# A seven-product output projection for the pooling layer, four units at a time

## The chip, the cores and the metric

The kernel runs on one core of a Trainium2 chip. The metric is the device time of one execution in microseconds (us); lower is better. A time is the median of several executions. The profile is one more execution, recorded by the hardware profiler. PE is the matrix engine, PEld its loading of weights, DVE the vector engine, ACT the scalar engine, POOL the general engine, and SP the queue that issues every transfer here.

## The reference, cut to what matters

Two pre-norm residual layers over 4096 tokens of width 1024: first sliding-window attention, then a pooling mixer. The change lies in the second, apart from the preparation of its weights.

```python
def pool_layer(h, w_in, w_mix, scale, w_out):
    u, z = jnp.split(h @ w_in, [POOL_WIDTH], axis=-1)
    p = multiscale_pool(u)       # trailing means over 2/4/8/16 tokens, minus u
    m = jnp.einsum('bsgc,gcd->bsgd', p, w_mix).reshape(B, S, POOL_WIDTH) * scale
    return (m * jax.nn.silu(z)) @ w_out

# x = x + pool_layer(rmsnorm(x)); the result is rmsnorm(x, final_g)
```

## The kernel before, in words

Every fp32 matrix product is made of three passes: each factor is split into a high and a low part (`split_sb`, L133 on ACT and L134 on DVE; the high part is a rounded copy, the low part the difference), and high*high, high*low and low*high are added up in PSUM (`PASSES`). A product of 128 contracted rows, 128 output channels and 512 tokens is thus three matmuls.

**Stage A (attention)** goes over eight blocks of 512 tokens (`s` = 0 to 7; the last outputs run on into the start of what follows). Beside it, in blocks 2 to 7, four calls of `seven` per block (half a weight unit each) prepare the weights of the pooling layer: for `u` and `z` units they make the seven weight combinations of a two-by-two block product, split them and store them to HBM (`w7_...`); for the output units `o` they only split the weight and store it in four pieces (`wo_...`). One such half costs seven splits of 128x256, seven stores and four sums on POOL for `u` and `z`, and four splits and four stores for `o`. Their order is u, z, o for each of the four units, so that blocks 2 and 5 hold four of the first kind and blocks 3, 4, 6 and 7 two of each.

**Stage B (pooling)** goes over four groups `g` of 1024 tokens. Each has an in-phase and an out-phase.

The in-phase makes eight units of 256 channels (u3, z3, u2, z2, ... u0, z0) by a two-by-two block scheme with seven products in place of eight: the token halves t and the channel halves k of each pair `p` give the right-hand factors B11, T1, T2, T3, B21, B22, T4 (`factor_sum` makes the T by differences in place, `factor` splits the result into a `set_...` tile). One `product` is 12 matmuls (four pairs, three passes) over 512 tokens and needs one weight tile of 512 KB, `w7_load`. Five such tiles are in flight. Four products of a unit add up in one PSUM bank X, one after the other; ACT copies the bank to the tile `ct_...` after each stage (`snapshot`, L656; the last is `result`, L662) before the next product may write it, and DVE adds the banks Y and Z (L660). So the order within a unit is 1, (3 of the unit before), 6, 5, 7, 2, 4.

A finished `u` unit goes through `pooled` (L710, L715: one to four shifted sums and a difference), a finished `z` unit through `gated`: z + z*tanh(z/2) on ACT (L721) and DVE (L722), times half the pooled value (L723). The results lie in four `raw` tiles `ar`, one for each pair.

The out-phase takes them directly: for each pair the four quarters B11, B12, B21, B22 are split, and each of four units (o3 to o0) is four calls of `o_pair` with 24 matmuls each (two channel halves, two token halves, two contracted halves, three passes) into four PSUM banks. That is 96 matmuls per unit and 384 per group. `o_result` adds the bank to the residual x (L694, the residual loaded to a `ct` tile by `o_open` in two transfers of 512 KB per unit), squares it (L734) and adds up the squares (L735); `stored` writes the unit to HBM in one transfer of 1 MB. The next group's x is loaded meanwhile (`h_load`, tile `xr`), scaled and made into factors.

The final normalisation of a group runs piece by piece in the in-phase of the next: `final_piece` loads 256 KB (`fin`), scales it on DVE (L788) and stores it, 16 times. In the last group it happens at the end: the last unit is computed in three parts (`LASTP`: token half 0, then two quarters of token half 1), each normalised as it is done (`last_sum`, `last_rsqrt`, `last_spread`, `last_scale`).

What issues when is written out by hand: every step is an event with a planned time (`at(t, fn, ...)`), counted in product lengths (`PROD` = 2.73 us). Events are emitted in the order of time; in stage B the compiler's scheduler may still move an instruction ahead of one that is not ready by its own estimate. Each engine then works strictly in its order, and SP issues the transfers in its own order: a transfer that has to wait for a free buffer or for DVE holds up those behind it.

Of the kernel before, what the change touches and what calls it, by code (L numbers as in the profile page):

```python
# [20 lines left out]
G = 512  # L21
# [31 lines left out]
def trunk_kernel(ctx, tc, xt, xm, ng, w_a_in, sinks, w_a_out, wu_t, wmix, pscale, w_b_z, w_b_out, fg, out):  # L53
# [17 lines left out]
    wout = {}  # L71
# [447 lines left out]
    def seven_load(key, src, hf):  # L519
        if hf == 0 and key[0] == "o":  # L520
            wout[key[1]] = [dram.tile([128, 2, 2, UC], F32, name=f"wo_{key[1]}_{i}") for i in range(4)]
        elif hf == 0:
            wseven[key] = [dram.tile([128, 2, 2, 2, 128], F32, name=f"w7_{key[0]}{key[1]}_{i}") for i in range(7)]
# [5 lines left out]
    def seven(key, hf):  # L529
        raw = wraws.pop((key, hf))  # L530
        if key[0] == "o":
            for c in range(4):
                t = lp.tile([128, 2, UC], F32R, tag="sl", bufs=SLOTS["sl"], name=f"part_o{key[1]}_{hf}_{c}")
# [25 lines left out]
    PROD, PAIR = 2.73, 5.45  # L559
# [6 lines left out]
    def open_left():  # L566
        left.close()
        for name, kw in (("bl", {}), ("bp", dict(space=PSUM))):
            pl[name] = E(tc.tile_pool(name=name, bufs=1, side="left", reuse_waits="tile", **kw))
        pl["ucar"] = pl["bl"].tile([128, 4, 2, 16], F32, name="ucar")  # L570
# [3 lines left out]
        for j, w in enumerate(WINDOWS):  # L574
            for t in range(w - 1):
# [4 lines left out]
              setl=("bl", 8), ct=("bl", 2), wk=("bl", 1), th=("bl", 1), sq=("bl", 1), sr=("bl", 2), sl=("bl", 1),  # L580
# [17 lines left out]
    def factor_sum(g, name, p):  # L598
        ph = (g, "in")
# [14 lines left out]
    def factor(ph, name, p):  # L614
        late = p < 2 if ph[1] == "out" else name in ("T4", "B22")
        t = bt([128, 2, G], "setl" if late else "set", f"set_{ph[0]}{ph[1]}_{name}_{p}", F32R)
# [7 lines left out]
    def w7_load(u, i):  # L624
        src = wout[u[2]][i] if u[1] == "o" else wseven[u[1], u[2]][i - 1]
# [4 lines left out]
    def product(u, i):  # L630
        bank = {1: "X", 6: "X", 7: "X", 4: "X", 2: "Y", 5: "Z", 3: "Z"}[i]
        first = i in (1, 2, 5)
        if first:
            banks[u, bank] = bpsum(bank, f"{bank}_{u[0][0]}{u[1]}{u[2]}")
        ps, w = banks[u, bank], w7.pop((u, i))
        for a, p in enumerate(PAIRS):
            t = sets[u[0], RIGHT[i], p]
            for b, (wl, hl) in enumerate(PASSES):
                nc.tensor.matmul(ps, w[:, p // 2, wl, p % 2], t[:, hl], start=(first and a == 0 and b == 0),  # L639
# [25 lines left out]
    def o_open(u):  # L665
        g, j = u[0][0], u[2]
        if g < NP - 1:
            c = bt([128, 2, 16 + G2], "ct", f"ct_{g}o{j}")[:, :, 16:]
        else:
            c = bt([128, 2, G2], "raw", f"ct_{g}o{j}")  # L670
        cts[u] = c
        for t in range(2):
            nc.sync.dma_start(c[:, :, G * t:G * t + G], x1[2 * g + t][j])

    def o_rhs(u, p, k, hl, t):
        return sets[u[0], f"B{k + 1}{t + 1}", p][:, hl]

    def o_pair(u, a):
        p = PAIRS[a]
        if a == 0:  # L680
            for i, tag in enumerate(("X", "Y", "Z", "pt")):
                banks[u, i] = bpsum(tag, f"{tag}_{u[0][0]}o{u[2]}")
        w = w7.pop((u, p))
        for i in range(4):
            n, t = i // 2, i % 2
            for k in range(2):
                for b, (wl, hl) in enumerate(PASSES):
                    nc.tensor.matmul(banks[u, i], w[:, wl, k, 128 * n:128 * n + 128], o_rhs(u, p, k, hl, t),
                                     start=(a == 0 and k == 0 and b == 0), stop=(a == 3 and k == 1 and b == 2))

    def o_result(u, i):
        n, t = i // 2, i % 2
        b = blk(u, n, t)
# [301 lines left out]
    for g in range(NP):  # L995
# [92 lines left out]
        if g == NP - 1:  # L1088
            continue
# [75 lines left out]
```

## Time and profile before

| | |
|---|---|
| median of 3 runs | 2626.57 us (2622.93 to 2632.19) |
| profiled execution | 2624.14 us, span 2622.0 us |
| PE busy | 2535.1 us, 97% of the span |
| DVE busy | 1504.4 us, 57% |
| ACT busy | 1041.8 us, 40% |
| POOL busy | 580.8 us, 22% |
| moved by DMA | 626.05 MB, mean 239 GB/s |

The time of the profiled execution lies 2.1 us above its span; the span is what the views of the trace divide. Stage B begins at 1619.4 us. A row of a window gives, for each engine, its busy time and (x) its instructions, then the granted PE clock (1.00 is full speed), the mean busy share of the 16 DMA engines and the rate.

### The profile page before, as it was taken

Reading aid. Unit: us, or ns where it says so; the run is one execution under the profiler, and the core shown is the slowest. Engines: PE = TensorE matmul, PEld = TensorE weight load, DVE = VectorE, ACT = ScalarE, POOL = GpSimd, SP = SyncE. Lnnn points to the kernel's source line nnn. Section 1 sums busy time; section 2 is a strip of 40 time slices with the busy share of each in tenths; the row PEclk is TensorE's granted clock in tenths of the full one; section 3 lists DMA queues with packets and bytes.
Section 4 is the critical chain, followed back from the end, with each engine's and each line's share of the span. In section 5 each row is a group of like instructions: output and inputs, shape, how many; then the busy total and the mean of one; then the engine's idle time right before and its main releaser. Section 6 shows DMA issues by size and latency. Waiting matters only on the chain.

```text
span 2622.0 us, 34809 instructions
## 1 busy us (share of the span) xinstructions
PE 2535.1 (97%) x12604; PEld 2135.6 (81%) x12604; DVE 1504.4 (57%) x2281; ACT 1041.8 (40%) x2680; POOL 580.8 (22%) x883
## 2 busy tenths in 40 slices
PE   6999999999999999999999999999999999999997
PEld 5888888888888888888888887888877877887886
DVE  5366656466466466565565557546646655655544
ACT  4464544455454454554554543222313231332221
POOL 3553323343243334333333330000000000000000
PEclk9998999999999999999999999999999999999999
DMA  8853856877767867877767758666677668758752
GB/s 293 307 200 129 304 190 206 292 251 242 265 239 245 288 230 238 295 242 232 271 234 247 250 196 301 193 216 244 203 257 268 217 225 279 258 177 279 247 203 97
DMA packets 175191, 626.05 MB, mean 239 GB/s; under 512 B 23198, under 2 KB 33438, under 8 KB 145324
## 3 DMA queue, kind: packets, MB, share of 16 engines
q1 hardware_dynamic: 175020, 623.83, 70.2%
q8 instruction: 100, 1.64, 0.2%
q14 instruction: 71, 0.58, 0.1%
HBM read 489.47 MB, written 117.51 MB: 231 GB/s over the span
## 4 chain that ended last, share of the span: by engine, by line
PE 65%; DMA 18%; DVE 10%; ACT 3%; issue 2%; POOL 1%; SPq 1%; DVEq 0%; POOLq 0%; ACTq 0%
PE mm L278 25%; PE s L395 3%; DMA fin<-x 2%; PE mm L288 2%; PE X_0u L639 2%; DMA out<-fin 2%; PE X_0z L639 2%; PE po L449 1%; PE X_1u L639 1%; DMA xt<-in_xt 1%; PE pT L420 1%; PE X_1z L639 1%; DMA rsq<-rs 1%; DMA w<-wparts 1%; PE X_3u L639 1%
## 5 line engine op out<-in xcount | busy, mean ns | idle before, releaser
L278 PE MATMUL mm<-h,w 128*128 128x512 f32 x3456 | 846.0, 396 | 8.0 <-DVE sz L364 3.4
L278 PEld LDWEIGHTS mm<-h,w 128*128 128x128 f32 x3456 | 638.7, 190 | 136.6 <-DVE sz L364 3.9
L278 PE MATMUL mm<-a,w 128*128 128x512 f32 x1536 | 375.8, 395 | 8.6 <-DMA w<-wparts 8.5
L436 POOL TENSOR_SCALAR_AFFINE_SELECT m<-m 64x256 fp32r<-64x256 f32 x512 | 230.7, 451 | 587.5 <-ACT m L427 502.0
L278 PEld LDWEIGHTS mm<-a,w 128*128 128x128 f32 x1536 | 282.8, 189 | 67.5 <-DMA w<-wparts 10.6
L407 ACT ACTIVATE P<-s,mx 128x129 f32<-128x129 f32 x512 | 182.0, 370 | 112.0 <-DVE mx L404 109.8
L412 POOL TENSOR_TENSOR P<-P,sm 128x516 f32<-128x516 f32 x128 | 145.7, 1139 | 154.3 <-DVE sm L411 142.9
L766 POOL TENSOR_TENSOR rs<-ms,mhalf 128x4 f32<-128x4 f32 x7 | 7.0, 1007 | 743.0 <-DVE ms L765 743.0
L456 ACT COPY tmp<-po 64x256 f32<-64x256 f32 x256 | 94.2, 368 | 145.6 <-PE po L450 87.7
L395 PEld LDWEIGHTS s<-kt,q 128*128 128x128 f32 x1024 | 134.4, 194 | 14.7 <-ACT s L386 4.8
L457 DVE TENSOR_TENSOR o<-po,tmp 64x256 f32<-64x256 f32 x256 | 107.7, 421 | 58.8 <-ACT tmp L456 53.0
L395 PE MATMUL s<-kt,q 128*128 128x192 f32 x1024 | 138.0, 276 | 2.8 <-ACT s L386 1.9
L327 DVE SCALAR_TENSOR_TENSOR q<-mm,q 64x512 fp32r<-64x512 f32 x128 | 88.2, 689 | 76.6 <-ACT q L326 74.9
L326 ACT ACTIVATE q<-mm 64x512 fp32r<-64x512 f32 x128 | 75.8, 593 | 74.7 <-PE mm L278 44.9
L407 ACT ACTIVATION_READ_ACCUMULATOR P<-s,mx 128x1 f32 x512 | 104.6, 204 | 0.0
L428 DVE TENSOR_TENSOR m<-pT,m 128x512 fp32r<-128x512 f32 x128 | 87.7, 685 | 26.9 <-ACT m L427 26.0
L400 DVE COPY_PREDICATED s<-mask,s 128x256 f32<-128x256 int8 x128 | 54.3, 424 | 74.6 <-PE s L395 67.9
L288 PE MATMUL mm<-w,h 128*128 128x256 f32 x768 | 96.4, 284 | 0.0
L288 PEld LDWEIGHTS mm<-w,h 128*128 128x128 f32 x768 | 94.9, 193 | 0.5
L427 ACT CAST m<-pT 128x512 fp32r<-128x512 f32 x128 | 75.0, 586 | 42.1 <-PE pT L420 39.0
L404 DVE TENSOR_REDUCE mx<-s 128x4 f32<-128x516 f32 x128 | 88.7, 693 | 3.3
L788 DVE SCALAR_TENSOR_TENSOR fin<-fin,fg_sb,bco 128x512 f32<-128x512 f32 x48 | 36.0, 751 | 88.6 <-DMA fin<-x 86.5
(357 smaller groups left out, 4342.7 us busy)
## 6 DMA issues: line engine op xcount, KB each, us to landing
w<-wparts SPq DMA_DIRECT2D x196, 1024.0 KB, 6.6
wparts<-w SPq DMA_DIRECT2D x28, 1024.0 KB, 6.8
xt<-in_xt SPq DMA_DIRECT2D x32, 512.0 KB, 6.1
res<-in_xt SPq DMA_DIRECT2D x32, 512.0 KB, 7.3
x<-res SPq DMA_DIRECT2D x32, 512.0 KB, 10.2
xr<-x SPq DMA_DIRECT2D x32, 512.0 KB, 5.5
xm<-in_xm SPq DMA_DIRECT2D x28, 512.0 KB, 7.0
w_u<-part_u SPq DMA_DIRECT2D x56, 256.0 KB, 3.0
```

Of the source, the lines that this page charges most:

```text
L278: nc.tensor.matmul(ps[:, c], w[:, wl, k % 4, 128 * c:128 * c + 128], rhs(k, hl), start=(k == 0 and i == 0), stop=(k == NK - 1 and i == 2))
L288: nc.tensor.matmul(ps[:, b], hts[s, k][:, hl, 128 * b:128 * b + 128], wtiles[U, k // 4][:, wl, k % 4], start=(k == 0 and i == 0), stop=(k ...
L327: nc.vector.scalar_tensor_tensor(dst[64 - r:128 - r], src, -SCALE, f32(dst[r:r + 64]), op0=ALU.mult, op1=ALU.subtract)
L395: nc.tensor.matmul(ps[:, 2 * c + u, 2 - 2 * u:194 - 2 * u], qs[s, j][:, c, 2 * b + u].rearrange("p r x -> p (r x)"), kt[:, j, hl, t:t + 19 ...
L404: nc.vector.tensor_reduce(mx.rearrange("p (c u) -> p c u", c=2), view(ps, 1, [(512, 2), (319, 2), (1, 129)]), axis=AX.X, op=ALU.min)
L407: nc.scalar.activation(P[:, i, 0:129], view(ps, 1 + 512 * (i // 2) + 319 * (i % 2), [(1, 129)]), AF.Exp, bias=mx[:, i:i + 1], scale=-1.0, ...
L412: nc.gpsimd.tensor_mul(P[:, :, 0:129], P[:, :, 0:129], sm.unsqueeze(2).to_broadcast([128, 4, 129]))
L428: nc.vector.tensor_sub(m1[:, 1], pv, f32(m1[:, 0]))
L436: nc.gpsimd.affine_select(out=v[rows], in_=f32(mu[wr, u, l]).rearrange("p c (r q) -> p c r q", r=2), **after)
L456: nc.scalar.copy(tmp[d:d + 64], pv[e:e + 64, r])
L457: nc.vector.tensor_add(dst, pv[d:d + 64, r], tmp[d:d + 64])
L639: nc.tensor.matmul(ps, w[:, p // 2, wl, p % 2], t[:, hl], start=(first and a == 0 and b == 0), stop=(a == 3 and b == 2), skip_group_check= ...
```

## The change

1. The output units are made by the seven-product scheme too. `seven` prepares `o` like `u` and `z`; `o_pair` and `o_result` go. Each unit is seven calls of `product`, so a group's out-phase has 4 x 7 x 12 = 336 matmuls of 512 tokens.
2. All four output units go through the products together: 1 for o3, o2, o1, o0, then 2 for all four, then 5, 6, 7, 3, 4 (in the last group 1, 6, 5, 7, 3, 2, 4). The banks X and Z of the four units take the tags X, Y, Z and pt. DVE adds each bank to the residual directly (`o_add`, seven times per unit), so the residual must be there in four blocks by channel half and token half (`o_load`, 16 transfers of 256 KB; `o_store`, 16 of 256 KB).
3. The out-phase needs B11, T1, T2, T3, B21, B22, T4 of each pair: seven splits and four differences where there were four splits. Tables of planned times (`OUT_FACTORS`, `IN_FACTORS`, `LAST_FACTORS`) place them and the factors of the next group.
4. The in-phase takes u and z of a pair together, product by product: 1u 1z 6u 6z 5u 5z 7u 7z 2u 2z 3u 3z 4u 4z.
5. The gate uses the function SiLU on ACT and one product on DVE in place of Tanh and two operations.
6. Loads and stores of stage B that are not weights are tied behind the last weight load in SP's order (`behind_w7`).
7. The new tail: token half 1 is finished first and normalised under the remaining products; the last product (4) of token half 0 is done in two quarters of 256 tokens, each for all four units.

The diff, cut:

```diff
@@ seven_load, seven
-        if hf == 0 and key[0] == "o":
-            wout[key[1]] = [dram.tile([128, 2, 2, UC], ...) for i in range(4)]
-        elif hf == 0:
+        if hf == 0:
             wseven[key] = [dram.tile([128, 2, 2, 2, 128], ...) for i in range(7)]
...
-        if key[0] == "o":
-            for c in range(4):
-                t = lp.tile([128, 2, UC], F32R, tag="sl", ...)
-                split_sb(t[:, 0], t[:, 1], raw[:, c])
-                nc.sync.dma_start(wout[key[1]][2 * hf + c // 2][:, :, c % 2], f32(t))
-            return
@@ buffers
-              setl=("bl", 8), ct=("bl", 2), wk=("bl", 1), ...
+              setl=("bl", 8), ct=("bl", 3), wk=("bl", 1), ...
@@ factor
-        late = p < 2 if ph[1] == "out" else name in ("T4", "B22")
-        t = bt([128, 2, G], "setl" if late else "set", ...)
+        t = bt([128, 2, G], "setl" if name in ("T4", "B22") else "set", ...)
@@ w7_load
-        nc.sync.dma_start(f32(t), src)
+        queued["w7"] = nc.sync.dma_start(f32(t), src)
+    def behind_w7():
+        return tc.issue_after(queued["w7"].ins)
@@ product
+            tag = bank
+            if u[1] == "o":
+                tag = ("X" if u[2] > 1 else "Y") if bank == "X" else "Z" if u[2] > 1 else "pt"
@@ residual and result
-    def o_pair(u, a):
...
-    def o_result(u, i):
...
+    def o_load(g, n, t, j):
+        with behind_w7():
+            nc.sync.dma_start(held[g, j, n, t], x1[2 * g + t][j][:, n])
+    def o_add(u, n, t, bank, c0=0, c1=G):
+        b = held[u[0][0], u[2], n, t][:, c0:c1]
+        nc.vector.tensor_add(b, b, banks[u, bank][:, c0:c1])
+    def o_done(u, n, t, c0=0, c1=G):
+        b_square(g, j == 3 and n == t, b[:, c0:c1], t, c0, c1)
+    def o_store(g, j, n, t):
+        with behind_w7():
+            nc.sync.dma_start(x2[g][j][:, n, G * t:G * t + G], held[g, j, n, t])
@@ gated
-        nc.scalar.activation(th, z, AF.Tanh, scale=0.5)
-        nc.vector.scalar_tensor_tensor(z, th, 1.0, z, op0=ALU.add, op1=ALU.mult)
-        nc.vector.scalar_tensor_tensor(a, a, 0.5, z, op0=ALU.mult, op1=ALU.mult)
+        nc.scalar.activation(th, z, AF.Silu)
+        nc.vector.tensor_mul(a, a, th)
@@ tail
-    LASTP = ((0, 0, G), (1, 0, G // 2), (1, G // 2, G))
+    LASTP = ((1, 0, G), (0, 0, G // 2), (0, G // 2, G))
@@ plan
+    OUT_FACTORS = (("B11", -31.0, 1.5, -1.6), ("B21", -21.0, 1.5, 4.0), ("T1s", -15.0, 1.5, 0.0), ("T1", -14.9, 1.5, 0.1),
+                   ("T3s", -4.8, 0.7, 4.5), ("T2s", 4.9, 2.0, 12.0), ("T2", 5.0, 2.0, 12.1), ("T3", 14.0, 2.0, 20.0),
+                   ("T4s", 15.0, 2.0, 21.0), ("B22", 16.0, 2.0, 22.0), ("T4", 17.0, 2.0, 23.0))
+    IN_FACTORS = (("load", 23.0, 7.3), ("scale", 31.0, 7.3), ("B11", 32.0, 7.3), ("T1s", 46.0, 3.6), ("T1", 46.1, 3.6),
+                  ("T2s", 60.0, 2.0), ("T2", 60.1, 2.0), ("T3s", 73.0, 0.7), ("T3", 77.0, 1.0), ("T4s", 79.0, 0.7),
+                  ("B21", 82.0, 1.0), ("B22", 87.0, 1.0), ("T4", 92.0, 1.0))
+    OUT_BLOCKS = ((0, 0, "ct", 0.3, 6), (0, 1, "ct", 6, 22.5), (1, 1, "ct", 12, 24.5), (1, 0, "wk", 21, 28.5))
...
-        for x, u in enumerate(stream):
-            order = [1, 6, 5, 7, 2, 4] if prev is None else [1, 3, 6, 5, 7, 2, 4]
+        for j in PAIRS:
+            us = [(ph, kind, j) for kind in "uz"]
+            for i in (1, 6, 5, 7, 2, 3, 4):
+                for u in us:
+                    at(pos, product, u, i)
...
+        us = [(po, "o", j) for j in PAIRS]
+        for i in (1, 6, 5, 7, 3, 2) if last_g else (1, 2, 5, 6, 7, 3, 4):
+            for u in us:
+                at(pos, product, u, i)
...
+        if last_g:
+            for i in (1, 2):
+                for u in us:
+                    at(pos, product, u, 4, c0, c1)
+                    pos += 1.45
+                last_norm(pos, g, i)
```

The planned times of the tables are microseconds from the start of the out-phase: name, time for pair 3, step to the next pair, time for pair 0; a trailing s is the difference, the others the split. `OUT_BLOCKS` gives channel half, token half, buffer and, in products, the first load and the first store.

More of the change, by code (lines that the diff above doesn't have):

```diff
@@ L638, in product @@
             for b, (wl, hl) in enumerate(PASSES):
-                nc.tensor.matmul(ps, w[:, p // 2, wl, p % 2], t[:, hl], start=(first and a == 0 and b == 0),
+                nc.tensor.matmul(ps[:, c0:c1], w[:, p // 2, wl, p % 2], t[:, hl, c0:c1], start=(first and a == 0 and b == 0),
                                  stop=(a == 3 and b == 2), skip_group_check=True)
@@ L662, in result, with o_open @@
             nc.scalar.copy(blk(u, n, t), banks[u, "X"])
-    def o_open(u):
-        g, j = u[0][0], u[2]
[L667 to L676, printed above, removed]
-    def o_pair(u, a):
[L679 to L689, printed above, removed]
-    def o_result(u, i):
-        n, t = i // 2, i % 2
-        b = blk(u, n, t)
-        nc.vector.tensor_add(b, b, banks[u, i])
-        b_square(u[0][0], u[2] == 3 and n == 0, b, t)
+    held = {}
+    def o_open(g, n, t, tag):
+        if tag == "raw":
+            c = bt([128, 2, G2], tag, f"o{g}_{n}{t}")
+        else:
+            c = bt([128, 2, 16 + G2], tag, f"o{g}_{n}{t}")[:, :, 16:]
+        for j in PAIRS:
+            held[g, j, n, t] = c[:, j // 2, G * (j % 2):G * (j % 2) + G]
+    def o_load(g, n, t, j):
[5 more added lines that the diff above has]
+    def o_done(u, n, t, c0=0, c1=G):
+        g, j = u[0][0], u[2]
+        b = held[g, j, n, t]
+        b_square(g, j == 3 and n == t, b[:, c0:c1], t, c0, c1)
+    def o_store(g, j, n, t):
+        with behind_w7():
+            nc.sync.dma_start(x2[g][j][:, n, G * t:G * t + G], held[g, j, n, t])
     def pooled(u, n):
@@ L833, in last_rsqrt, with last_spread @@
         last[i] = rs
-    def last_spread(u, i):
+    def last_spread(g, i):
         t, c0, c1 = LASTP[i]
@@ L996, in trunk_kernel @@
         ph = (g, "in")
-        stream = [(ph, kind, j) for j in PAIRS for kind in "uz"]
         if g == 0:
```

252 lines of the change are left out of this document (121 added, 131 removed).

## Prediction

> **What bounds the kernel now.** I read the head of the page and its chain first, then a table of windows cut at the stages, then the waits of PE in stage B, then the groups of DVE and ACT in one group of tokens, and the transfers last.
>
> ```profile
> span 2622.0 us, 34809 instructions
> PE 2535.1 (97%) x12604; PEld 2135.6 (81%) x12604; DVE 1504.4 (57%) x2281; ACT 1041.8 (40%) x2680; POOL 580.8 (22%) x883
> PE 65%; DMA 18%; DVE 10%; ACT 3%; issue 2%; POOL 1%; SPq 1%; DVEq 0%; POOLq 0%; ACTq 0%
> ```
>
> PE is busy for 97% of the span and carries 65% of the chain: a matmul less is time less, where nothing else is late. The stages, each group's in-phase and out-phase in turn and the tail last:
>
> ```profile
> core 0: us, PE busy (x) PEld busy (x) DVE busy (x) ACT busy (x) POOL busy (x), PEclk, DMA share, GB/s
> 1619.40:1773.70 154.30, 154.10 (x672) 127.20 (x673) 82.60 (x100) 40.51 (x72) 0.81 (x26) 0.99 0.66 211
> 1773.70:1861.40 87.70, 87.70 (x389) 72.61 (x388) 59.52 (x84) 29.56 (x49) 0.00 (x0) 1.00 0.59 207
> 1861.40:2025.40 164.00, 156.49 (x677) 127.25 (x676) 88.62 (x105) 39.15 (x70) 2.99 (x3) 0.99 0.77 255
> 2025.40:2113.00 87.60, 87.60 (x389) 72.54 (x388) 59.40 (x84) 29.15 (x49) 0.00 (x0) 1.00 0.59 207
> 2113.00:2272.20 159.20, 154.76 (x675) 125.81 (x674) 88.24 (x104) 38.29 (x68) 1.98 (x2) 1.00 0.80 263
> 2272.20:2359.80 87.60, 87.60 (x388) 72.55 (x387) 59.51 (x84) 29.25 (x49) 0.00 (x0) 1.00 0.59 206
> 2359.80:2515.60 155.80, 153.76 (x675) 125.93 (x674) 87.97 (x103) 38.20 (x68) 2.02 (x2) 1.00 0.79 265
> 2515.60:2605.72 90.12, 90.12 (x454) 76.80 (x452) 29.61 (x44) 13.59 (x22) 1.01 (x1) 1.00 0.29 99
> 2605.72:2622.00 16.28, 2.91 (x12) 2.37 (x12) 9.99 (x26) 0.75 (x2) 1.39 (x2) 0.65 0.66 243
> ```
>
> The out-phases have PE busy all the way at full clock: nothing is late in them. The in-phases differ (154 to 164 us) at equal work, so they hold waits.
>
> ```profile
> 1771.21 2.72 PE X_0z L639 x12
> L688 PE MATMUL X_1o<-set_1out_B,w_1o 128*128 128x512 f32 x96 | 24.4, 389 | 0.0
> PE X_1z L639 <- ACT ct_1z L656: 3.4, 1, 3.4
> PE X_1z L639 <- DMA w_1z<-w_z: 2.6, 2, 2.3
> ```
>
> From the chain: twelve matmuls of 512 take 2.72 us, 0.227 each (389 ns is one with its pipeline). An in-phase of 56 products is then 152.3 us, an out-phase of 384 matmuls 87.0, as the windows show. Above 152.3 lie 2.0, 11.7, 6.9 and 3.5 us; about 1 us of each of the last three is the matmuls of the squares' sums, so waits are some 2, 10.5, 6 and 2.5, 21 in all. The waits quoted are two of them: a bank copied late by ACT, a weight tile landed late.
>
> **The change, part by part.**
>
> *Output products.* 336 matmuls per group for 384: 48 x 0.227 = 10.9 us, and 43.5 over four groups, all on the path.
>
> *What pays for them on DVE and ACT.* Per group 12 more splits, 16 differences and 12 more bank additions (28 for 16).
>
> ```profile
> L134 DVE TENSOR_TENSOR set_1out_B<-ar,set_1out_B 128x512 fp32r<-128x512 f32 x16 | 10.5, 686 | 0.6 <-ACT set_1out_B L133 0.6
> L694 DVE TENSOR_TENSOR ct_1o<-ct_1o,X_1o 128x512 f32<-128x512 f32 x4 | 2.8, 688 | 18.2 <-PE X_1o L688 18.2
> 2055.18 1.90 DVE L608 TENSOR_TENSOR xr<-xr 128x512 f32<-128x512 f32 x3
> L723 DVE SCALAR_TENSOR_TENSOR ar<-ar,ct_1z 128x1024 f32<-128x1024 f32 x8 | 9.8, 1222 | 0.1
> L133 ACT CAST set_1out_B<-ar 128x512 fp32r<-128x512 f32 x16 | 9.8, 623 | 7.8 <-PE Z_1z L639 2.8 <-PE X_1z L639 2.3 <-DVE ar L723 2.2
> L721 ACT ACTIVATE th<-ct_1z 128x1024 f32<-128x1024 f32 x8 | 8.5, 1061 | 14.3 <-DVE ct_1z L660 13.8 <-DVE ct_1z L722 0.5
> ```
>
> Three in a row take 1.90, so one in a run costs 0.60 (1.90 less 0.69, halved). 40 x 0.60 = 24 us more on DVE; the gate loses one operation of eight times 1.22 = 9.8. DVE goes from 59.4 + 88.6 = 148 to about 162 us in a group of 228: 71%, no bound on average. ACT gains 12 x 0.62 = 7.4.
>
> By stretches it is tighter. In the first 33 us of the out-phase the plan puts on DVE: pooled and gate left over from the last pair (3.7), about 29 splits and differences (17.4), the additions of products 1 and 2 with their squares (11 x 0.60 = 6.6), one scaling (1.3), and gaps where a split waits for ACT's copy right behind its difference (five or six of 0.7): about 33. So DVE is full there and runs up to 7 us behind. Who waits: product 5 of a unit takes the bank that product 2 left three products earlier, 8.2 us; lag nearly uses that up. At the start, product 1 needs the low part of B11 of pair 0 2.3 us in; counted from the end of product 3u (pooling 2.5, gate with ACT 2.9, differences, split) it is there after 3. I take 1 + 1 us per group for the two; bounds 0 (the scheduler fills the gaps: in the old out-phases DVE was full for 40 us as well and PE lost nothing) and 6.
>
> *Transfers in the out-phase.* Before, 16 weight tiles, now 28. In MB: 28 x 0.524 = 14.7; residual 16 x 0.262 = 4.2; next x 8 x 0.524 = 4.2; 12 of the 16 stores 3.1; 26.2 in 76.2 us, 344 GB/s where there were 207.
>
> ```profile
> 1650.00:1690.00 40.00, 40.00 (x178) 33.13 (x177) 21.03 (x23) 7.93 (x15) 0.00 (x0) 1.00 0.62 195
> 2020.00:2044.00 24.00, 24.00 (x107) 19.88 (x107) 22.52 (x27) 9.37 (x14) 0.00 (x0) 1.00 0.94 343
> 2150.00:2190.00 40.00, 36.86 (x160) 29.59 (x159) 23.64 (x26) 6.62 (x13) 0.00 (x0) 1.00 0.85 283
> w_1o<-wo SPq DMA_DIRECT2D x16, 512.0 KB, 3.6
> fin<-x SPq DMA_DIRECT2D x16, 256.0 KB, 5.9
> ```
>
> Weights alone stream at 195 GB/s without a wait; 343 GB/s held for 24 us with PE full; but 283 with small pieces among them went with 3 us of PE idle. So 344 is at the edge. The plan's worst stretch is 22 to 44 us in, where x comes (3.1 MB) beside residual (1.6), stores (0.5) and weights (4.2): 9.4 MB, against 7.5 at 343: 1.9 MB or 5.5 us of backlog. A weight tile asked for when its buffer comes free has 4 products, 10.9 us, and takes 3.6 to 6 now. SP adds to it: a store behind a late DVE, or x waiting for a `raw` buffer that the last split has not let go, holds the weights behind it by the 3 to 7 us of lag. The next group's x, loaded from the first microseconds of the out-phase on before, now comes 23 to 45 us in; its first reader is the scaling at 31, PE needs it at 76, so that costs nothing while the phase has 30 us to spare. I take 1 us per group; bounds 0 (all fits, as at 343) and 16 (the whole phase at 283 is 92.6 us). The last group stores nothing and loads no next x; 2 us of waits there for its tighter banks.
>
> The Trainium skill speaks against the smaller pieces: "DMA: Bandwidth & Descriptors", Measured (HBM→SBUF, 128 partitions), tells one to batch to 1 MiB or more, since each transfer pays about 2 us before its bytes. By its formula 256 KB would take 2.6 us alone and 32 such pieces in a row 83 us (an estimate), more than the whole phase, which would make rival (c) of it. The trace disagrees for transfers that overlap: 343 GB/s with 512 KB ones.
>
> *In-phase.* Two units at a time give each bank three products between its copy and its next writer, save two places: after product 1, and at the end of a pair, where 1u of the next pair takes the bank that 4u left one product (2.72) before. The chain there, for pair 3 with four shifted sums:
>
> ```profile
> L710 DVE TENSOR_TENSOR sums<-sums 128x1037 f32<-128x1037 f32 x6 | 7.4, 1238 | 0.2
> L656 ACT COPY ct_1z<-X_1z 128x512 f32<-128x512 f32 x12 | 7.0, 585 | 12.9 <-PE X_1z L639 12.8
> ```
>
> From the end of 3u: addition 0.7, pooling 5 x 1.24 = 6.2, addition for z 0.7, SiLU 1.06 on ACT, and only behind it in ACT's order the copy of the bank, 0.59: 9.4 us at best, where 1u comes 8.2 after; 1.2 lost per group. Pair 2 just fits, pairs 1 and 0 have room. `fin` stays as it was, one every 7 us with DVE waiting for its landing: another 1.5 in each of three groups. 2 us at the start of group 0 stay (its first weight tile). 5 + 4.5 + 2 = 12 for 21: I take -9. Bounds: -19 (all but the start go) and +5 (pair ends lose twice as much).
>
> *Gate function.*
>
> ```profile
> L89 ACT ACT_TABLE_LOAD x1 | 1.3, 1283 | 0.8 <-PEq L1152 0.8
> ```
>
> One load of a function table served Exp, Tanh, Square and copies so far. SiLU is not among them: at least one load more, 1.3 us before a copy with 2.7 of room; I take +1 (0 to 3).
>
> The Trainium skill ("ScalarE: Activation LUTs", What ACT_TABLE_LOAD costs) gives 1283 ns for the load, as the row, and 1380 more for draining, 2.66 per switch: +1.4 to this term. Its Table sets section has the cheap functions in every set, by which one switch is all; no run here shows that for SiLU.
>
> *Weights of `o` in stage A.* Eight halves become of the costlier kind, two in each of blocks 3, 4, 6, 7. The key's copies mark the blocks:
>
> ```profile
> L308 ACT CAST kt<-mm x8: 577/582/582, 622.7 to 818.1; 64x512 fp32r<-64x512 f32 x8
> L308 ACT CAST kt<-mm x4: 579/581/585, 1005.3 to 1009.3; 64x512 fp32r<-64x512 f32 x4
> L308 ACT CAST kt<-mm x4: 578/582/583, 1199.0 to 1203.0; 64x512 fp32r<-64x512 f32 x4
> L308 ACT CAST kt<-mm x4: 581/582/584, 1392.6 to 1396.7; 64x512 fp32r<-64x512 f32 x4
> ```
>
> By the last copies, block 4 (mixed) took 191.2, block 5 (all of the costly kind) 193.7, block 6 (mixed) 193.7: 0 to 2.5 per block, which takes in the six more splits, eight sums on POOL and six more stores of such a block; I take 1.25 x 4 = +5 (0 to 10).
>
> *Tail.* After the last matmul 16.3 us remain.
>
> ```profile
> 2602.45 5.35 DVE L848 SCALAR_TENSOR_TENSOR ct_3o<-ct_3o,fg_sb,bcl 128x512 f32<-128x512 f32 x8 [2.21 <-PE bcl L839]
> 2607.79 0.74 DVE L814 TENSOR_TENSOR ct_3o<-ct_3o,last 128x256 f32<-128x256 f32 x2
> ```
>
> The last additions wait 2.1 us (2605.7 to 2607.8) behind the scaling of the first token half; that scaling moves ahead of 20 us of products. -2 (bounds -4 and +2, eight stores for four).
>
> *Sum,* on the profiled execution of 2624.1: -43.5 products, +6 and +2 out-phases, -9 in-phases, +1 table, +5 stage A, -2 tail, which is -40.5: 2583.6. The median of the runs is 2.5 above that execution; I say 2586.
>
> **Rivals.**
> (a) *The plan holds everywhere:* no waits in the out-phases, in-phases at 152.3 plus the start. -43.5 - 19 - 2 + 1 + 3 = -60: 2566. For it: the old out-phases lost nothing with DVE full. Against: the chain at pair 3 and the `fin` pieces.
> (b) *DVE and transfers take half:* 6 us for DVE and 2 for transfers in each of three out-phases and 2 in the last, stage A at its upper end, in-phases as they were: -43.5 + 26 + 10 + 1 - 2 = -8.5: 2618; with stage A at 5 and in-phases 5 better, 2608. For it: DVE is full for 33 us. Against: banks leave 8.2 us of room.
> (c) *Transfers become the bound of the out-phases, and it gets slower:* the 26.2 MB come at 283 GB/s, 92.6 us for 87.6 before, +5 in three groups; the last group's gain of 12.9 and +6 of stage A and table leave +8: 2635. It decides at 299 GB/s (26.2 MB in 87.6 us). For it: the row at 283 with small pieces. Against: 343 over 24 us, and weights have 10.9 us of room.
> (d) *SiLU's table has no copy:* two loads of 1.28 around each of 32 SiLUs, 82 us of ACT; at 16 pair ends some 3 us reach PE: +48, 2634. Against: one load served four functions.
>
> **How the numbers follow.** What a measurement of this kernel can tell from no change is about 0.3%, 8 us. Chances: the forecast (2570 to 2606) 0.72, (a) 0.13, (b) 0.09, (c) 0.04, (d) 0.02. The predicted time is the forecast's, 2586. The range leaves out (c), (d), most of the upper part of (b) and half of (a): 2564 to 2609. Faster than 2618.7: the forecast, (a) and nearly all of (b), 0.92; same 0.04; slower 0.04.
>
> **What would show it.** Out-phases of 77 to 80 us with 336 matmuls, DMA near 340 GB/s in them, DVE above 80% in their first 30 us; 24 more stores of weight parts in blocks 3, 4, 6 and 7, each of these up to 2.5 longer; in-phases of 154 to 157 with waits at pair 3's end; one more table load; less than 15 us after the last matmul. It is wrong if the out-phases show PE waiting for weight tiles (c), if many table loads stand in ACT's rows (d), or if in-phases lengthen because ACT sits behind DVE at each pair's end.

## The result, and the profile after

| | before | after |
|---|---|---|
| median | 2626.01 us, 4 runs (2622.93 to 2632.19) | 2579.55 us, 4 runs (2571.16 to 2582.96) |
| ratio | | 0.9831, 95% interval 0.9808 to 0.9854 |
| profiled execution | 2624.14 us | 2582.96 us |

The change gained 46.5 us by the medians, 41.2 between the two profiled executions. The prediction said 2586 us, so the total was met. Two of its terms were not, in opposite directions.

The head of the page after, and the windows cut at the stages (same columns as before):

```profile
PE 2490.3 (96%) x12412; PEld 2096.5 (81%) x12412; DVE 1575.2 (61%) x2437; ACT 1067.9 (41%) x2755; POOL 606.5 (23%) x915
0.00:1634.40 1634.40, 1562.65 (x8286) 1329.85 (x8287) 955.65 (x1575) 789.63 (x2256) 596.22 (x879) 0.99 0.73 249
1634.40:1788.60 154.20, 152.78 (x674) 125.89 (x673) 80.85 (x102) 42.29 (x75) 0.81 (x26) 1.00 0.62 202
1788.60:1864.80 76.20, 76.20 (x338) 63.13 (x337) 64.90 (x99) 30.40 (x54) 0.00 (x0) 1.00 0.93 328
1864.80:2024.60 159.80, 156.48 (x680) 128.19 (x679) 94.75 (x123) 40.95 (x76) 3.03 (x3) 0.99 0.80 250
2024.60:2100.70 76.10, 76.10 (x338) 63.03 (x337) 65.94 (x99) 30.98 (x55) 0.00 (x0) 1.00 0.97 349
2100.70:2257.80 157.10, 154.17 (x677) 126.52 (x676) 93.96 (x121) 39.96 (x74) 2.01 (x2) 1.00 0.79 253
2257.80:2334.00 76.20, 76.20 (x338) 63.12 (x337) 65.67 (x99) 30.93 (x55) 0.00 (x0) 1.00 0.97 347
2334.00:2488.50 154.50, 153.78 (x678) 127.01 (x677) 96.71 (x125) 41.96 (x77) 2.01 (x2) 1.00 0.82 262
2488.50:2568.05 79.55, 79.52 (x405) 67.95 (x404) 49.26 (x83) 20.43 (x37) 1.70 (x2) 1.00 0.71 240
2568.05:2581.20 13.15, 2.40 (x14) 1.86 (x12) 7.51 (x20) 0.42 (x1) 0.69 (x1) 0.65 0.47 160
```

The first row of the same table for the kernel before:

```profile
0.00:1619.40 1619.40, 1560.11 (x8286) 1332.56 (x8286) 938.96 (x1554) 783.33 (x2234) 570.58 (x847) 0.99 0.73 248
```

By row against before: the four out-phases have PE full, window for window, and are 45.0 us shorter together (11.5, 11.5, 11.4 and 10.6). The in-phases are 625.6 us for 633.3, which is 7.7 less. The tail is 3.1 shorter. Stage A is 15.0 longer: PE is busy there 2.5 us more and idle 12.5 more. The sum, -45.0 - 7.7 - 3.1 + 15.0 = -40.8, is the difference of the spans.

### The profile page after: what moved, and what is told of

The parts are those of the page before. It is cut to its first block, busy times and chain, and to the rows that moved or that the text cites. A ratio compares the mean times of both kernels' runs of the same rounds, so it can differ in the third digit from the quotient of the medians.

```text
span 2581.2 us, 35131 instructions
## 1 busy us (share of the span) xinstructions
PE 2490.3 (96%) x12412; PEld 2096.5 (81%) x12412; DVE 1575.2 (61%) x2437; ACT 1067.9 (41%) x2755; POOL 606.5 (23%) x915
## 4 chain that ended last, share of the span: by engine, by line
PE 55%; DMA 20%; DVE 13%; ACT 5%; issue 4%; POOL 1%; SPq 1%; DVEq 0%; POOLq 0%; ACTq 0%
PE mm L277 19%; DMA xt<-in_xt 2%; DMA w<-wparts 2%; PE s L394 2%; DMA fin<-x 2%; ACT P L406 2%; PE X_2o L638 2%; PE X_1o L638 2%; DMA rsq<-rs 2%; PE X_3o L638 2%; PE X_0z L638 2%; PE X_3u L638 1%; PE X_3z L638 1%; PE X_0u L638 1%; PE X_0o L638 1%
## 5 line engine op out<-in xcount | busy, mean ns | idle before, releaser
L394 PEld LDWEIGHTS s<-kt,q 128*128 128x128 f32 x1024 | 133.2, 193 | 21.4 <-DVE q L326 8.4
```

The costliest lines, as they stand in the source:

```text
L394: nc.tensor.matmul(ps[:, 2 * c + u, 2 - 2 * u:194 - 2 * u], qs[s, j][:, c, 2 * b + u].rearrange("p r x -> p (r x)"), kt[:, j, hl, t:t + 19 ...
```

## The experiments

All ratios are to the kernel before, which was timed again beside each group of runs, with 95% intervals; "stage B at" is the time at which its first product starts in the profiled execution.

### Stage A: what made it longer

Three kernels take the preparation of `o` apart. **e1** is the kernel before with the seven-part preparation of `o` and nothing else of the change:

```diff
-            for c in range(4):
+            # four sums on POOL
+            for c in range(7):
...
+                    nc.sync.dma_start(x, f32(t))   # parts 5 to 7: stored, read by nobody
```

> The kernel before with one part of the change alone: in stage A the output weights are prepared like the others (seven splits, seven stores and four sums per half in place of four and four; three of the parts are stored where nobody reads them). Stage A was 15 us longer after the change (1619.4 to 1634.4 us), where 5 was forecast. Theory S (the preparation of the output weights costs it): start of stage B at 1631 to 1637 and a time of 2638 to 2644, ratio 1.005 to 1.007. Rival P (the planner of stage A laid out everything anew, and the preparation itself costs the 5 of the forecast): 1622 to 1626, ratio 1.001 to 1.003.

Measured: 2631.87 us against 2622.84, ratio 1.0035 (1.0017 to 1.0052), stage B at 1631.9. The preparation alone costs 9.2 us by the ratio (4.5 to 13.6). One profile against one gives 12.5. The ratio lies between the two expectations; the start of stage B is where S had it.

**e2** is the changed kernel with four splits per half of `o`, no sums, and all seven stores, three of them of a part stored already. **e3** has all splits and sums and only the first four stores:

```diff
e2  +        if key[0] == "o":
    +            for i, m in enumerate((v[:, 0, 0], v[:, 1, 0], v[:, 0, 1], v[:, 1, 1])):
...
    +                nc.sync.dma_start(wseven[key][i][:, hf], f32(t))
    +                if i > 0:
    +                    nc.sync.dma_start(wseven[key][3 + i][:, hf], f32(t))
...
e3  +            if key[0] != "o" or i < 4:
                     nc.sync.dma_start(wseven[key][i][:, hf], f32(t))
```

> The changed kernel with four splits per half of an output weight and no sums, but all seven stores (three of them store a part again; the output weights are not the right ones, so the output is not the reference's). If the stores hold up SP's queue (theory Q), stage A stays near 1630 to 1635 us and the time near 2575 to 2582. If the splits and sums on ACT, DVE and POOL, and SP's waiting for DVE's splits, are what costs (theory W), stage A falls to 1619 to 1624 and the time to 2565 to 2570.

> The changed kernel with seven splits and four sums per half of an output weight, but only four stores (products 5, 6 and 7 of the output units read parts 1, 2 and 3 again, so the output is not the reference's). Theory Q (the stores): stage A falls to 1619 to 1624 us and the time to 2565 to 2570. Theory W (the engines' work): stage A stays at 1630 to 1635 and the time at 2575 to 2582. Half each if both share it.

Measured: e2 2561.42 us, ratio 0.9778 (0.9752 to 0.9805), stage B at 1613.6. e3 2565.07 us, ratio 0.9784 (0.9752 to 0.9817), stage B at 1620.1. Taking away either the splits with their sums or the stores recovers the cost (the interval of e3 just overlaps that of the changed kernel, 0.9808 to 0.9854), so neither the splits' time nor the bytes are it alone. Two things then suggested themselves that need both a split and its store; their letters are not those of e1, e2 and e3. They are: SP, which stands at a store until DVE has made the part, with weight loads behind it (theory S); and ACT, which cannot cast part i+2 before store i has landed, since the parts have two buffers (theory Q). The waits of stage A in the changed kernel (total us, times, longest), SP's first:

```profile
SPq L543 <- DVE part_o L133: 101.8, 37, 9.5
```

(98.7 for the parts of u and 90.5 for those of z, 291.0 together), then ACT's for stores to land and PE's for weight tiles:

```profile
ACT part_z L132 <- DMA w_z<-part_z: 32.7, 13, 6.1
ACT part_o L132 <- DMA w_o<-part_o: 26.3, 14, 5.5
ACT part_u L132 <- DMA w_u<-part_u: 24.0, 10, 5.6
PE mm L277 <- DMA w<-wparts: 17.5, 13, 2.5
```

and, of the kernel before, the two of them that differ most:

```profile
SPq L535 <- DVE part_o L134: 57.6, 20, 7.5
PE mm L278 <- DMA w<-wparts: 8.7, 9, 3.5
```

**e5** spreads the seven parts over time, with the store planned 4 us behind its split; **e6** issues the stores from POOL:

```diff
e5  +                for p in range(7):
    +                    at(t + 0.9 + 0.4 * p, seven_part, k, hf, p)
    +                    at(t + 0.9 + 0.4 * p + 0.3, seven_store, k, hf, p)
e6  -            nc.sync.dma_start(wseven[key][i][:, hf], f32(t))
    +            nc.gpsimd.dma_start(wseven[key][i][:, hf], f32(t))
```

> The changed kernel with the seven parts of a half block prepared one at a time, 5.5 us apart instead of in a burst, and each part's store put into SP's order 4 us behind its split (for all three weights u, z and o). Same splits, same sums, same bytes, same number of stores. Theory S (stage A's 15 us are SP standing at stores that wait for DVE, with the next weight tile's load behind them): a store finds its split done, weight loads go out on time, PE's waits for weight tiles of stage A fall from 17.5 us to 14 or less, stage B starts at 1614 to 1623 us instead of 1634.4, and the time is 2560 to 2570 us, ratio to the kernel before 0.975 to 0.980. Theory W (the splits' own time on DVE and ACT, or the bytes): nothing of that is less, stage B starts at 1630 to 1637 and the ratio stays at 0.982 to 0.986.

> The changed kernel with the seven parts' stores issued by POOL instead of SP; splits, sums, their order and the bytes as they are. Theory S (SP held by stores): SP has no part store before its weight loads; stage B starts at 1614 to 1625 us and the time is 2560 to 2572, unless POOL, which then waits for DVE at each store, comes late with its sums and low halves, which would show as waits of PE or ACT for POOL. Theory W (the splits themselves, or the bytes): stage B starts at 1630 to 1637 as now, time 2577 to 2586.

Measured: e5 2582.02 us, 0.9831 (0.9811 to 0.9850), stage B at 1635.2. The edit did not do what it was for: SP waited 128.2 + 128.2 + 122.1 us for the three kinds of parts, where it had been 291.0. So e5 tells nothing about S. e6 2604.96 us, 0.9920 (0.9889 to 0.9951), stage B at 1658.2. PE no longer waits for a weight tile at all in stage A, and yet it is 24 us longer. PE's two longest waits there:

```profile
PE s L394 <- DVE sm L410: 20.0, 5, 4.8
PE s L394 <- ACT s L385: 17.4, 9, 5.3
```

and ACT's for stores to land:

```profile
ACT part_u L132 <- DMA w_u<-part_u: 66.5, 19, 8.5
ACT part_z L132 <- DMA w_z<-part_z: 65.8, 20, 7.5
ACT part_o L132 <- DMA w_o<-part_o: 61.8, 22, 7.5
```

ACT waits 194 us for the stores to land where it was 83, and the attention's own work on ACT and DVE comes late. POOL, too, now stands 190 us at stores whose part DVE has not made; PE's listed waits for POOL did not grow by it (12.5 us for 13.4). That spoke for Q, and the number of buffers tests it. **e9** is the changed kernel unaltered, as the measure beside the next two. **e10** lets every third part use the stage's `sr` buffer (three in turn); **e11** gives the parts of `o` that one buffer alone:

```diff
e10 +            tag = ("sl", "sl", "sr")[i % 3]
e11 +            tag = "sl" if key[0] != "o" else "sr"
```

> The changed kernel once more, unaltered, as the measure for the three beside it. Kernels whose stage A is the same instructions started stage B at 1634.4, 1638.1, 1628.4 and 1623.4 us, so one profile says little about a few us; medians are to be compared. Expected: ratio to the kernel before 0.981 to 0.985, stage B at 1623 to 1638.

> The changed kernel with three buffers in turn for the seven parts of a half block (every third one takes the stage's sr buffer) instead of two; splits, stores, bytes and engines as they are. Theory Q (the cost in stage A goes round a ring: ACT's cast of part i+2 waits for the store of part i to land, that store waits in SP's order, and meanwhile what ACT and DVE owe to PE is late): ACT's waits for part stores to land, 83 us in stage A of the changed kernel (32.7 for z, 26.3 for o, 24.0 for u), fall to half or less, stage B starts 5 to 15 us earlier than that of the unaltered kernel beside it, and the time falls by 5 to 15 us. Rival S (SP alone: weight loads standing behind stores that wait for DVE): the stores wait for DVE as before, so time within 3 us of the unaltered kernel.

> The changed kernel with a single buffer (the stage's sr) for the parts of o in place of two in turn; u and z keep their two. Nothing else changes. Theory Q (the ring through two buffers): each part of o now waits for the store before it to land, ACT's waits for stores of o rise from 26 us to 60 us or more, stage B starts 8 to 25 us later than in the unaltered kernel beside it and the time is longer by as much. Rival S (SP alone): a store still follows its split as before and SP only sees them further apart; within 4 us of the unaltered kernel.

Measured: e9 2578.26 us, 0.9817 (0.9792 to 0.9841), stage B at 1635.7. e10 2572.99 us, 0.9796 (0.9773 to 0.9820), stage B at 1623.4. e11 2579.12 us, 0.9827 (0.9802 to 0.9852), stage B at 1634.4. In e11 the waits did what was intended. ACT's for stores of `o`, SP's for parts of `o` and PE's for weight tiles in e9:

```profile
ACT part_o L132 <- DMA w_o<-part_o: 30.2, 12, 5.1
SPq L543 <- DVE part_o L133: 102.0, 36, 9.3
PE mm L277 <- DMA w<-wparts: 21.4, 12, 4.2
```

and in e11:

```profile
ACT part_o L132 <- DMA w_o<-part_o: 65.1, 27, 7.2
SPq L544 <- DVE part_o L133: 142.6, 39, 9.5
PE mm L277 <- DMA w<-wparts: 12.7, 9, 3.7
```

ACT's went from 30.2 to 65.1 us and SP's from 102.0 to 142.6, and the median moved by 0.9 us, below the 8 to 25 that Q asked for (each ratio is known to some 6.5 us). So Q fell for `o`. The rival's number, within 4 us, came true, but its mechanism is no better off: SP stood 41 us more at stores of `o` with no loss that the medians show. e10 is the fastest of the kernels that leave nothing out, 5.3 us below e9, but its interval overlaps e9's, and ACT's waits for stores hardly fell in sum (98.9 us for 105.3).

What is shown: the preparation of `o` costs about 9 us alone, and both its parts are needed for the cost. Which hold carries it is open. PE's own wait for weight tiles goes along with it loosely: in the eleven executions with these stores in SP's order and two buffers, from 8.7 us (stage B at 1619.4, before) over 11.7 (1613.6, e2) and 15.8 (1623.8, e12) to 17.5 (1634.4, after) and 21.4 (1635.7, e9), but e5 has 14.5 at 1635.2. That is a correlation and no cause.

### In-phase: two units at a time, fin, and the gate

**e4** puts back the old order of the in-phase, one unit after the other; with it the factor B22 goes behind T4 and pooling starts with the other half:

```diff
-        for j in PAIRS:
-            us = [(ph, kind, j) for kind in "uz"]
...
+        stream = [(ph, kind, j) for j in PAIRS for kind in "uz"]
...
+            order = [1, 6, 5, 7, 2, 4] if prev is None else [1, 3, 6, 5, 7, 2, 4]
```

> The changed kernel with the in-phase in the old order, one unit at a time (and the planned times of B22 and T4 of the next group exchanged, as that order needs them). The four in-phases are 625 us in all now, 633 before. Theory I (two units at a time shortens the waits for copied banks): 632 to 640 us in all, time 2586 to 2595. Rival (the waits come from the final pieces and the weights, whatever the order): 622 to 628, time 2577 to 2583. About 2.7 us per group may be added at the start of each out-phase, since product 3 of the last unit comes later; that is to be read apart.

Measured: 2587.77 us, 0.9886 (0.9847 to 0.9925); in-phases 152.6, 165.5, 162.9 and 160.1, 641.1 in all. PE's longest wait in e4's in-phases:

```profile
PE X_1u L638 <- ACT ct_1u L655: 6.1, 4, 2.8
```

and in the changed kernel's:

```profile
PE X_1u L638 <- ACT ct_1u L655: 2.1, 1, 2.1
```

Two units at a time are worth 15.5 us of these windows against the changed kernel's 625.6; by the ratios some 14, with intervals that overlap. The execution that was profiled is e4's slowest, 15.7 us above its median, so the windows are a rough measure. PE's listed waits there are 18.9 us for 8.3: at a bank that ACT has not copied yet 13.9 for 7.9, and at one that DVE has not added yet 4.0 for none. PE's own busy time is 623.2 us for 617.2, at a clock of 0.99 in the last two phases for 1.00.

**e8** issues the load of a finished piece 5 us ahead of its scaling:

```diff
+                at(pos + 23.0 + 7.0 * i, final_load, g - 1, jj, n, t)
                 at(pos + 28.0 + 7.0 * i, final_piece, g - 1, jj, n, t)
```

> The changed kernel with the loads of the finished pieces (fin, one each 7 us of an in-phase) issued 5 us ahead of the DVE scaling that reads them, where both now stand together and DVE waits 3.5 to 5.7 us for the landing. Theory F (what is left above 154 us in the second and third in-phase is DVE, and ACT behind it, held by these landings): in-phases of 159.8, 157.1, 154.5 us become 155 to 157, 154 to 156 and 154, the time falls by 4 to 8 us, ratio to the kernel before 0.979 to 0.9825. Rival G (it is the pooling chain at the pairs' ends, whatever fin does): in-phases unchanged within 1 us each, ratio 0.982 to 0.985.

Measured: 2587.91 us, 0.9856 (0.9833 to 0.9878); in-phases 154.2, 162.8, 161.7, 160.3, which is 639.0 for 625.6. Neither theory had them longer (by the ratios, 6.6 us with overlapping intervals). DVE's wait for the landings in the changed kernel:

```profile
DVE fin L784 <- DMA fin<-x: 104.1, 34, 5.8
```

and in e8:

```profile
DVE fin L789 <- DMA fin<-x: 99.7, 37, 7.8
```

It is nearly as large as before, so issuing earlier did not take the wait away; why was not found. What grew is PE's wait at the pairs' ends for a bank's last copy (L661), from 3.0 us to 11.5.

That a landing can reach PE is seen in one place of the changed kernel, 1904 to 1912 us. DVE stands 3.53 us for a piece, the gate's product comes behind it, ACT's next SiLU waits for that product until 1910.13, the bank's copy stands behind the SiLU in ACT's order, and PE waits for the copy:

```profile
1904.60 0.75 DVE L784 SCALAR_TENSOR_TENSOR fin<-fin,fg_sb,bco 128x512 f32<-128x512 f32 x1 [3.53 <-DMA fin<-x]
1911.71 4.32 PE L638 MATMUL X_1u<-set_1in_T,w_1u 128*128 128x512 f32 x12 [2.07 <-ACT ct_1u L655]
```

How much of the in-phases all the landings hold stays open.

**e12** puts back Tanh and its two DVE operations in the gate:

```diff
-        nc.scalar.activation(th, z, AF.Silu)
-        nc.vector.tensor_mul(a, a, th)
+        nc.scalar.activation(th, z, AF.Tanh, scale=0.5)
+        nc.vector.scalar_tensor_tensor(z, th, 1.0, z, op0=ALU.add, op1=ALU.mult)
+        nc.vector.scalar_tensor_tensor(a, a, 0.5, z, op0=ALU.mult, op1=ALU.mult)
```

> The changed kernel with the gate as it was before: Tanh of half the argument and two DVE operations for one SiLU and one product, 8 times a group. Theory I (the gate stands at the pair's end ahead of a bank's copy): 1.2 us more on DVE at each pair's end, in-phases 2 to 6 us longer each where pair 3 and 2 have no room, together 6 to 14 us more, and one table load less (1.3 us). Rival J (the gate has room): time within 3 us of the unaltered kernel beside it, or 1 us less for the table load saved.

Measured: 2582.99 us, 0.9834 (0.9812 to 0.9857), 4.7 above e9 with overlapping intervals. The second to fourth in-phase of e9:

```profile
1866.20:2024.20 158.00, 154.87 (x680) 126.93 (x679) 94.25 (x123) 41.11 (x76) 3.03 (x3) 1.00 0.79 251
2100.40:2254.60 154.20, 153.63 (x678) 126.86 (x677) 95.22 (x122) 41.23 (x75) 2.02 (x2) 1.00 0.81 261
2330.80:2484.90 154.10, 153.65 (x677) 126.83 (x677) 96.78 (x125) 42.11 (x77) 2.01 (x2) 1.00 0.82 263
```

and of e12:

```profile
1855.60:2016.70 161.10, 156.25 (x680) 128.23 (x679) 102.45 (x131) 41.85 (x76) 3.03 (x3) 0.99 0.79 254
2093.10:2252.70 159.60, 155.51 (x678) 127.96 (x677) 101.61 (x129) 40.53 (x74) 2.01 (x2) 0.99 0.80 254
2329.20:2488.50 159.30, 155.53 (x678) 127.96 (x677) 103.44 (x132) 41.54 (x75) 2.01 (x2) 0.99 0.80 254
```

DVE has 6 to 8 us more per phase and the phases are 3.1, 5.4 and 5.2 longer, 14.6 over all four, at the upper end of theory I's 6 to 14. Against the other execution of the changed kernel, with in-phases of 625.6 for e9's 620.7, it is 9.7. Of the 13.7 in these three phases 5.1 is PE's own busy time, at a clock of 0.99 for 1.00. In the medians it is not separable, since e12's stage A, the same instructions as e9's, was 11.9 us shorter in its profiled execution. So by these windows the gate, whose only term in the prediction's sum was a table load, is a good part of the in-phases' gain: with Tanh they stand at 635.3, no better than before.

### Out-phase: is 349 GB/s the limit?

**e7** repeats each residual load as a copy from memory to memory that nothing reads:

```diff
             nc.sync.dma_start(held[g, j, n, t], x1[2 * g + t][j][:, n])
+            nc.sync.dma_start(dram.tile([128, G], F32, name=f"again{g}_{j}_{n}_{t}"), x1[2 * g + t][j][:, n])
```

> The changed kernel with each residual load of an out-phase (16 of 256 KB) followed by a further copy of the same 256 KB from memory to memory that nothing reads: 4.2 MB read and 4.2 MB written more in each of the four out-phases. The transfers then ask for about 400 GB/s in an out-phase of 76.2 us (30.4 MB moved once) where they now get 347 to 349 at a busy share of 0.97. Theory L (349 GB/s at 0.97 is the transfers' limit and the out-phase just fits): each of the first three out-phases grows to 83 us or more with PE waiting for weight tiles w7, together +20 us or more, ratio to the kernel before 0.990 or more. Theory M (the busy share of 0.97 is a queue kept full ahead of need, with room left): out-phases stay at 76 to 78.5 us, time within +6 us of the changed kernel, ratio 0.981 to 0.9855.

Measured: 2592.64 us, 0.9870 (0.9849 to 0.9890). The first three out-phases:

```profile
1782.50:1860.30 77.80, 76.57 (x337) 62.93 (x336) 63.15 (x96) 28.81 (x51) 0.00 (x0) 1.00 0.95 357
2024.50:2102.80 78.30, 76.73 (x337) 62.92 (x336) 62.69 (x94) 28.99 (x51) 0.00 (x0) 1.00 0.97 357
2262.30:2341.10 78.80, 76.77 (x338) 62.93 (x337) 63.02 (x94) 29.24 (x52) 0.00 (x0) 1.00 0.98 365
```

and PE's waits from stage B's start on:

```profile
PE ms L744 <- ACT sr L132: 9.2, 3, 3.3
PE X_2o L638 <- DMA w_2o<-w_o: 2.0, 2, 1.4
PE X_1o L638 <- DMA w_1o<-w_o: 1.6, 2, 1.2
PE X_0o L638 <- DMA w_0o<-w_o: 1.2, 1, 1.2
```

The out-phases grew by 1.6 to 2.6 us and PE began to wait for output weights, 4.8 us in all, at 357 to 365 GB/s. The in-phases after them grew by 10.4 together: PE's idle time in them by 4.5, with a new wait of 9.2 for the sum of the squares (`ms`), which ACT had not made ready, and less of others; its busy time by 5.9, at clocks of 0.97, 0.98 and 0.99 where they were 0.99, 1.00 and 1.00. M had the phases nearly right and the total wrong, L the direction.

So 347 to 349 GB/s was not the limit. A phase's mean hides its middle, where the next x comes beside residual and weights. Here are 40 us of it in the second out-phase, of the changed kernel and of e7:

```profile
2042.00:2082.00 40.00, 40.00 (x178) 33.14 (x177) 29.84 (x44) 9.08 (x16) 0.00 (x0) 1.00 1.00 379
2048.00:2088.00 40.00, 38.43 (x168) 31.19 (x168) 26.39 (x38) 6.10 (x11) 0.00 (x0) 1.00 1.04 409
```

In the three out-phases these 40 us had 377 to 379 GB/s with PE full, and in e7 408 to 410 with all of PE's waits for output weights inside. The best 20 us had 407 to 413 with PE full and 415 to 417 in e7. Whether the DMA engines or the copies ahead of the weights in SP's order made PE wait there was not tested. "Perfetto Trace Analysis" of the Trainium skill (Engine Utilization) has a single core going above its 358 GB/s share, up to about 435 for its 16 DMA engines; the 409 and the 417 agree with both.

## Why the prediction was right, and where it was not

| term | predicted | measured in the profiled pair |
|---|---|---|
| out-phases: products and their waits | -43.5 + 8 | -45.0 |
| in-phases | -9 | -7.7 |
| table load | +1 | 0, hidden |
| stage A | +5 (0 to 10) | +15.0; 9.2 by e1's ratio |
| tail | -2 | -3.1 |

- **Output products: right.** 336 matmuls take 76.2 us at full clock, with PE full all the way. The four windows fell by 45.0 us for 43.5 of products.
- **DVE in the out-phase: full, but done sooner; the lag did not come.** In each of the three out-phases DVE works with hardly a pause for the first 25 us and then stands until the next group's x has landed, 33 to 34 us in. So it is busy 24.6, 25.6 and 25.4 us of the first 33, and the sign "DVE above 80%" was missed with 74 to 78%. Here are the first of these windows and the end of the pause:

```profile
1788.60:1821.60 33.00, 33.00 (x147) 27.36 (x146) 24.58 (x40) 13.50 (x23) 0.00 (x0) 1.00 0.86 290
1822.48 2.48 DVE L778 SCALAR_TENSOR_TENSOR xr<-xr,ng_sb,bch 128x1024 f32<-128x1024 f32 x2 [8.96 <-DMA xr<-x]
```

  The working had 33 us: 29 of work and 4 of gaps in which a split waits for ACT. The gaps did not come, as other work stood between a difference and its split; 25 splits and differences fell into the window for 29, and the scaling came at its end or later. So the step "runs up to 7 us behind" failed, and with it the 2 us a group: PE waits for nothing in the out-phases. Rival (b), whose place this was, fell too.
- **Transfers in the out-phase: rate right, price not.** 344 GB/s was foreseen, 328 to 349 came, and the 1 us a group was not paid. The step that failed is the worst stretch, 22 to 44 us in, for which the working took 343 GB/s as all there is and a backlog of 5.5 us: the stretch moved 389, 389 and 383 GB/s with PE full. What came late was x, and PE had room for that, as the working said. Rival (c) asked for 299 GB/s or less. The rule of "DMA: Bandwidth & Descriptors" in the Trainium skill (Measured (HBM→SBUF, 128 partitions): batch to 1 MiB), measured there on transfers issued from GpSimd and not from SP, would by the prediction's estimate of 83 us have made the 256 KB pieces the bound; the rows disagree for transfers that overlap.
- **The sum of the waits.** By the working's own terms, 2 and 1 us in each of three groups and 2 in the last, the out-phases' waits are 11 us and not the 8 of the sum, which makes 2589. The out-phases paid none of it.
- **Stage A: mis-sized, the one term that went against the forecast.** The step read block lengths off one profile and took 1.25 us a block. By the last of the key's copies, blocks 4, 5 and 6 took 195.6, 201.5 and 197.6 us for 191.2, 193.7 and 193.7.

```profile
L307 ACT CAST kt<-mm x8: 578/581/582, 620.0 to 818.2; 64x512 fp32r<-64x512 f32 x8
L307 ACT CAST kt<-mm x4: 578/580/582, 1009.8 to 1013.8; 64x512 fp32r<-64x512 f32 x4
L307 ACT CAST kt<-mm x4: 579/582/582, 1211.3 to 1215.3; 64x512 fp32r<-64x512 f32 x4
L307 ACT CAST kt<-mm x4: 576/580/582, 1408.9 to 1412.9; 64x512 fp32r<-64x512 f32 x4
```

  But such lengths cannot price a block: block 5, whose preparation did not change, took from 193.1 to 201.5 us in six executions of this same stage A (the changed kernel, e4, e7, e8, e9, e12). In these six, stage B started between 1623.4 and 1638.1, at 1630.6 in the mean, so the +15.0 is one execution too. The 9.2 of e1 is the better figure, at the edge of the bounds.
- **In-phase: size right, place half right.** PE's listed waits fell from 16 us to 8. Behind pair 3's end they are 2.1, 0.7 and 0.7, but 1.0 and 2.0 stand at the end of pair 2, which was said to just fit; the scheduler put z's addition between the pooling sums, which shortens the chain that was worked out. That 7.7 hid two things was not foreseen: by the windows the new order (e4, 15.5) and the shorter gate (e12, 9.7 to 14.6) are each worth more than it, and either one taken back gives all of it away.
- **Table load: one, as said, but free.** It stands at 1667.56 in front of a SiLU that waited for DVE anyhow. Of the draining that "ScalarE: Activation LUTs" in the Trainium skill adds (What ACT_TABLE_LOAD costs), no run shows anything: 1.64 us of waiting covers it. Rival (d) fell: one load served SiLU with all copies and squares.

```profile
1667.56 1.28 ACT L716 ACT_TABLE_LOAD   x1
1670.49 1.06 ACT L716 ACTIVATE th<-ct_0z 128x1024 f32<-128x1024 f32 x1 [1.64 <-DVE ct_0z L659]
```

So the main term, the removed products, was right with its mechanism. That the total came within 1 us of the sum in the profiled pair is luck: the out-phases came 9.5 us better and stage A 10 us worse than said. The median of the runs lies 6.5 us below the forecast.

## What to carry to other kernels

Where PE is full in a stage, cost its removed matmuls in full, and spend the doubt on the work that moves to a stage with waits. Extra steps that are small on every engine can cost there when each of them ties several engines together in order, and taking away any one link may free it all: measure the whole step alone (e1), and do not argue it from one engine's waits, which grew by 35 to 41 us in e11 at no cost that the medians show. An operation on the chain at the end of a scheduled phase can cost time though its engine is idle for much of that phase: DVE was busy for some 60% of the in-phases after the first, and one operation of 1.2 us more in each gate, eight in an in-phase, made the four in-phases 10 to 15 us longer in single profiles (4.7 by the medians, with overlapping intervals). And a mean rate or a mean share over a phase can hide its order: DVE was full for 25 us and then stood, and the transfers had their peak in the middle.

## What the runs showed of the hardware that was not expected

- Transfers of 256 and 512 KB issued from one queue kept 347 to 349 GB/s for 76 us with PE full at clock 1.00, 377 to 379 for 40 us and 407 to 413 for 20 us of it. With more asked for (e7), 408 to 410 came for 40 us, and PE waited for tiles.
- In the second to fourth in-phase, nearly the same matmuls keep PE busy longer where PE also waits longer: 462.2 us busy with 4.1 idle (e9), 464.4 with 7.0 (after), 467.3 with 12.7 (e12), 469.4 with 15.4 (e8), 470.3 with 11.5 (e7), 470.6 with 17.9 (e4), at granted clocks from 1.00 in e9 down to 0.97, 0.98 and 0.99 in e7. These go together; no run shows which causes which.
- The same instructions of stage A ended 14.7 us apart in six executions at mean clocks of 0.985 to 0.990, while the first three out-phases of stage B took 76.0 to 76.5 us in all kernels that leave them alone. One profile is no measure for a stage that lives on waits.
